# Two address homes for the streamed weight pieces of a fused hybrid layer

## The chip, the cores and the metric

The kernel runs on one core of one Trainium2 chip. The metric is the device time of one launch in microseconds. The profile, the trace and every row below come from one execution of the kernel, taken by the hardware profiler. The names of its engines are PE (TensorE matmul), PEld (TensorE weight load), DVE (VectorE), ACT (ScalarE), POOL (GpSimd) and SP (SyncE).

## The reference

One layer with 256 tokens of width 2048. A wide projection feeds four branches (a gated linear recurrence, dilated attention in three groups, RWKV-7, and a convolution with layer norm); their outputs are gated, projected back to width 2048, weighted by sigmoids of a fifth slice of the projection, summed, projected by `w_out`, added to the input and normalized.

```python
h = jnp.einsum('bsd,de->bse', x, w_in) + b_in
(a_x, a_gate, q, k, v, b_gate, c_r, c_k, c_v, c_wd, c_ad, c_gate,
 d_val, d_glu, d_gate, merge_logits) = jnp.split(h, split_points, axis=-1)
y_a = ...   # depthwise conv, block gates, linear scan
y_b = ...   # dilated window attention, 3 groups x 4 heads
y_c = ...   # RWKV-7 scan, 8 heads of 64
y_d = ...   # depthwise conv of 31 taps, layer norm, silu
merge_g = jax.nn.sigmoid(merge_logits).reshape(bsz, s, N_BRANCH, D_MODEL)
mixed = jnp.zeros_like(x)
for n in range(N_BRANCH):
    mixed = mixed + merge_g[:, :, n] * jnp.einsum('bsc,cd->bsd', ys[n] * jax.nn.silu(gates[n]), w_br[n])
out = jnp.einsum('bsd,de->bse', mixed, w_out)
return _layernorm(ALPHA * x + out, ln_g, ln_b)
```

All data is float32. The kernel splits each float32 operand of the large projections into two parts of the type float32r (`h`, and `l` for what is left) and adds three products: h by h, h by l and l by h.

## The kernel before, in words

The weights (w_in, w_br and w_out, some 185 MB) are streamed once, in pieces of 512 KB: 128 partitions by 1024 float32. `split` handles one piece. SyncE issues the load into a tile `raw`, ScalarE casts it to `wh` (L208), and VectorE computes `wl` = raw - wh (L209, shown in the trace as L65, the line of a helper that records VectorE's instructions). The cast and the subtraction are traced with a priority 400 instructions ahead of their place in the program. `raw` has four tiles, `wh` and `wl` have three each, all in the pool `wp`.

A piece is used in one of two ways. In `channel_major` and `opening`, `multiply` (L229) takes 128 columns of the piece as the stationary operand and moves 256 tokens of x; a piece gives 24 matmuls. In `token_major` (L279), 128 tokens of x (or of a gated branch output, or of the mixed sum) stand, and 512 columns of the piece move; a piece gives 12 matmuls (w_out's fourth chunk: 24 with 256 columns).

The two parts of x are `xh` and `xl` in the pool `xp`, which also holds the gated branch outputs `yh` and `yl`; later the tiles of xh and xl hold the two parts of the mixed sum. The pools are placed in address order as they are opened: `cp` (constants), `ap` (tags `mx4`, `tt`, `pad`), `wp`, `xp`, `bp` (all other tiles, with twelve tiles of the tag `rk`). The streamed weights thus lie directly below x. The last 256 columns of w_out are an exception: their parts `lasth` and `lastl` are `rk` tiles in `bp`, above x, and move over the standing mixed sum (L1056).

The order of the projections is fixed by the program: the opening, then channel-major up to the gate `ga` (to 182 us in the trace), token-major `merge(0)` (to 306), channel-major `gd`, token-major `merge(3)` (329 to 450), channel-major `gc`, q and k (to 626), token-major v, channel-major `gb` (692 to 717), then token-major to the end: `merge(2)`, `merge(1)`, w_out. Each change from one kind to the other is called a handover below; there are seven.

The branches are generators in the queue `side`; `pump` runs some of their steps after each piece, against a budget. Their VectorE instructions keep program order. The instructions of each engine are put in order by a scheduler when the program is built, and a tile waits for the release of the tile whose place it takes.

`tt` has five tiles. Its users are, in program order: u, th, gi, rd, rs (the linear recurrence), acc, sh, sl, csq, sh, sl (the convolution branch), the gates ga, gd, gc, gb, the outputs yc and yb, and at the end four tiles `z`, which GpSimd loads with x for the residual.

Of the kernel before, what the change touches and what calls it, by code (L numbers as in the profile page):

```python
# [19 lines left out]
P = 128  # L20
T = 256
# [52 lines left out]
def tile_hybrid(  # L74
# [8 lines left out]
    ap = ctx.enter_context(tc.tile_pool(name="ap", bufs=1))  # L83
    wp = ctx.enter_context(tc.tile_pool(name="wp", bufs=1))
    xp = ctx.enter_context(tc.tile_pool(name="xp", bufs=1))
    bp = ctx.enter_context(tc.tile_pool(name="bp", bufs=1))
    pss = ctx.enter_context(tc.tile_pool(name="pss", bufs=4, space=PSUM))
    psb = ctx.enter_context(tc.tile_pool(name="psb", bufs=4, space=PSUM))
# [2 lines left out]
    def big(tag, bufs, name, dt=F32):  # L91
        pool = ap if tag in ("mx4", "tt") else xp if tag in ("yh", "yl") else bp
        return pool.tile([P, NJ, T], dt, tag=tag, name=name, bufs=bufs)

    def tt(name, dt=F32):
        return big("tt", 5, name, dt)

    def rk(name, dt=F32):
        return big("rk", 12, name, dt)
# [99 lines left out]
        pump(1e12)  # L199


    def split(src, c0, n, k, nk, queue=None):
        raw = wp.tile([P, nk, n], F32, tag="raw", name="raw", bufs=4)
        (queue or nc.sync).dma_start(raw, src[:, k : k + nk, c0 : c0 + n])
        h = wp.tile([P, nk, n], F32R, tag="wh", name="wh", bufs=3)
        l = wp.tile([P, nk, n], F32R, tag="wl", name="wl", bufs=3)
        with tc.high_priority(offset=AHEAD):
            S.copy(h, raw)  # L208
            V.tensor_tensor(l, raw, h.bitcast(F32), op=ALU.subtract)  # L209
        return h, l  # L210
# [27 lines left out]
    def channel_major(src, nk, c0, n, rh, rl, budget):  # L238
        ps = columns(n)
        for k0, kn in pieces(nk, n):  # L240
            multiply(ps, *split(src, c0, n, k0, kn), k0, kn, nk, rh, rl)
            pump(budget * n * kn / (512 * KP))
        return ps

    def opening(cols, budget):

        pss_ = [columns(512) for _ in cols]
        for k0, kn in ((0, 1), (1, 1)) + tuple((k, KP) for k in range(2, KT, KP)):
            xs = load_x(k0, kn)
            for n, (c0, ps) in enumerate(zip(cols, pss_)):  # L250
                early = S if k0 < 2 and n == 0 else None
                if k0 == 0 and n == 0:
                    parts_ = [split(w_in_r, c0 + q * T, T, 0, 1, early) for q in range(2)]
                    split_x(xs, k0, kn)
                    for q, (h, l) in enumerate(parts_):
                        multiply(ps[0 : 2 * q + 2], h, l, 0, 1, KT, xh, xl, 2 * q)
                    continue
                h, l = split(w_in_r, c0, 512, k0, kn, early)
                if n == 0:
                    split_x(xs, k0, kn)  # L260
                multiply(ps, h, l, k0, kn, KT, xh, xl)
                pump(budget * kn / KP)
        return pss_
# [7 lines left out]
    def token_major(src, nk, c0, lh, ll, budget, n=512):  # L271
        ps = [pss.tile([P, 512], F32, tag="ps", name="ps") for _ in range(2)]
        for k0, kn in pieces(nk, n):
            h, l = split(src, c0, n, k0, kn)
            for t in range(2):
                for k in range(kn):
                    kk = k0 + k
                    for i, (a, w) in enumerate(((lh, h), (ll, h), (lh, l))):
                        PE.matmul(  # L279
                            ps[t][:, 0:n],  # L280
                            a(kk, t),
                            w[:, k, :],
                            start=(kk == 0 and i == 0),
                            stop=(kk == nk - 1 and i == 2),
                        )
            pump(budget * n * kn / (512 * KP))
        return ps
# [50 lines left out]
    def lru(ax, sps, res):  # L338
        (sp8,) = sps
        u = tt("u")  # L340
        for j in range(NJ):
            V.tensor_scalar(u[:, j, :], ax[:, j, :], col(PK_CONV + 3, j), col(PK_CONVB, j), op0=ALU.mult, op1=ALU.add)
            for back in range(1, 4):
                o = u[:, j, back:T]
                V.scalar_tensor_tensor(o, ax[:, j, 0 : T - back], col(PK_CONV + 3 - back, j), o, op0=ALU.mult, op1=ALU.add)
            yield 1300
        th = tt("th")
        gi = tt("gi")
        for j in range(NJ):
            ps = bank("psg")  # L350
            PE.matmul(ps[:, 0:T], bd[0][:, j, :], u[:, j, :], start=True, stop=True)
            PE.matmul(ps[:, T:], bd[1][:, j, :], u[:, j, :], start=False, stop=True, skip_group_check=True)
            S.activation(th[:, j, :], ps[:, 0:T], AF.Sigmoid, bias=col(PK_GAB, j))
            S.activation(gi[:, j, :], ps[:, T:], AF.Sigmoid, bias=col(PK_GXB, j))
            yield 0
        rd = tt("rd")
        rs = tt("rs")
        for j in range(NJ):
            V.tensor_scalar(th[:, j, :], th[:, j, :], sp8[:, j : j + 1], None, op0=ALU.mult)
        yield 800  # L360
        S.activation(rd, th, AF.Exp, scale=-1.0)
        S.activation(th, th, AF.Tanh, scale=0.5)
        V.tensor_scalar(rd, rd, 0.5, 0.5, op0=ALU.mult, op1=ALU.add)
        V.scalar_tensor_tensor(rs, th, 1.0, rd, op0=ALU.add, op1=ALU.mult)
        yield 1700
        V.scalar_tensor_tensor(rd, rs, 2.0, rd, op0=ALU.subtract, op1=ALU.mult)
        yield 1100
        V.tensor_scalar(rs, th, 1e-33, None, op0=ALU.max)
        S.activation(rs, rs, AF.Sqrt)
        V.tensor_tensor(u, gi, u, op=ALU.mult)  # L370
        yield 1700
        V.scalar_tensor_tensor(th, th, 1e17, rs, op0=ALU.mult, op1=ALU.min)
        yield 1100
        V.scalar_tensor_tensor(th, th, -2.0, rd, op0=ALU.mult, op1=ALU.mult)
        yield 1100
        V.tensor_tensor(u, u, th, op=ALU.mult)
        yield 1100
        V.tensor_scalar(rd, rd, -2.0, -1.0, op0=ALU.mult, op1=ALU.add)
        yield 600
        y = gi  # L380
        for j in range(NJ):
            V.tensor_tensor_scan(y[:, j, :], rd[:, j, :], u[:, j, :], 0.0, ALU.mult, ALU.add)
        yield 1400
        res.append(y)
# [13 lines left out]
    def conformer(cu, res):  # L398
        acc = tt("acc")
        for w in range(31):  # L400
            for j in range(NJ):
                if w == 0:
                    V.tensor_scalar(acc[:, j, :], cu[:, j, 0:T], col(PK_DW, j), col(PK_DWB, j), op0=ALU.mult, op1=ALU.add)
                else:
                    V.scalar_tensor_tensor(
                        acc[:, j, :], cu[:, j, w : w + T], col(PK_DW + w, j), acc[:, j, :], op0=ALU.mult, op1=ALU.add
                    )
                yield 400
        ps = bank("psm")
        total(ps, parts(acc, tt))  # L410
        mean = bp.tile([P, T], F32, tag="s1", name="mean", bufs=4)
        S.activation(mean, ps[:, 0:T], AF.Copy, scale=1.0 / BW)
        V.tensor_tensor(acc, acc, mean[:, None, :].to_broadcast([P, NJ, T]), op=ALU.subtract)
        sq = tt("csq")
        S.activation(sq, acc, AF.Square)
        yield 1100
        ps = bank("psv")
        total(ps, parts(sq, tt))
        rstd = bp.tile([P, T], F32, tag="s1", name="rstd", bufs=4)
        S.activation(rstd, ps[:, 0:T], AF.Sqrt, bias=eps_ln, scale=1.0 / BW)  # L420
        V.reciprocal(rstd, rstd)
        V.tensor_tensor(acc, acc, rstd[:, None, :].to_broadcast([P, NJ, T]), op=ALU.mult)
        yield 1500
        for j in range(NJ):
            S.activation(sq[:, j, :], acc[:, j, :], AF.Sigmoid, bias=col(PK_CB, j), scale=col(PK_CG, j))
            V.tensor_scalar(acc[:, j, :], acc[:, j, :], col(PK_CG, j), col(PK_CB, j), op0=ALU.mult, op1=ALU.add)
        V.tensor_tensor(acc, acc, sq, op=ALU.mult)
        yield 1900
        res.append(acc)
# [528 lines left out]
    merge(1, *yhb, False, True)  # L958


    z = [[tt("z").rearrange("p a b -> p (a b)") for _ in range(2)] for _ in range(2)]
    for t in range(2):
        for i in range(2):
            G.dma_start(z[t][i], x[t * P : (t + 1) * P, i * 1024 : (i + 1) * 1024])
# [77 lines left out]
        for t in range(2):  # L1042
            residual(t, i, c0, n, ps[t])
    for k in range(0, KT, 4):
        raw = wp.tile([P, 4, T], F32, tag="raw", name="raw", bufs=4)
        nc.sync.dma_start(raw, w_out_r[:, k : k + 4, DM - T :])
        S.copy(lasth[k // 4], raw)
        V.tensor_tensor(lastl[k // 4], raw, lasth[k // 4].bitcast(F32), op=ALU.subtract)
# [98 lines left out]
```

## Time and profile before

| what | value |
| --- | --- |
| three runs | 1057.39, 1058.17, 1058.19 us; median 1058.17 us |
| the profiled execution, its own time | 1057.35 us |
| span from its first to its last instruction | 1055.6 us |
| TensorE busy | 1042.8 us |
| VectorE busy | 722.2 us |
| ScalarE busy | 497.0 us |
| mean granted TensorE clock | 0.995 |
| read from HBM | 198.98 MB |

The span is what the trace covers; the execution's own time has 1.75 us more around it. Busy time of TensorE counts pipelined matmuls with modelled ends, so the pace of a stream is better read from how long a run of so many matmuls takes in the chain of waits. That chain goes back from the last instruction, at each step to what released it or to the instruction before it on its engine.

### The profile page before, as it was taken

What the parts mean: (1) busy time and instruction counts of PE and PEld (TensorE: products, weight loads), DVE (VectorE), ACT (ScalarE), POOL (GpSimd) and SP (SyncE); (2) the same over time, 40 slices, a digit from 0 to 9 for tenths busy, and PEclk for the clock granted to TensorE, in tenths of its full rate; (3) what the DMA queues carried; (4) which work ended last, traced back from release to release, by engine and by line L of the source; (5) the groups of instructions that cost most, each with busy time, mean ns of one, the idle gap of its engine ahead of it and who ended that gap; (6) DMA issues with size and microseconds to landing.
All of it is one profiled execution on the core that took longest, in us unless ns stands there. A gap on an engine that the chain in (4) does not pass through costs nothing.

```text
span 1055.6 us, 16618 instructions
## 1 busy us (share of the span) xinstructions
PE 1042.8 (99%) x6669; PEld 921.2 (87%) x6669; DVE 722.2 (68%) x985; ACT 497.0 (47%) x594; POOL 41.4 (4%) x75
## 2 busy tenths in 40 slices
PE   7999999999999999999999999999999999999997
PEld 6999999887789877899999998898888888888886
DVE  5769988999969996665544444556666565556656
ACT  3365445557734435434544443346565444345341
POOL 0010000000020020000100000000000000000000
PEclk9999999999999999999999999999999999999998
DMA  8885766665686677555866666664556667676662
GB/s 279 247 254 155 204 187 186 189 183 150 186 215 187 199 206 200 182 154 151 288 180 181 182 187 189 194 183 142 170 154 209 209 202 206 207 226 199 193 192 89
DMA packets 108174, 203.11 MB, mean 192 GB/s; under 512 B 8436, under 2 KB 17296, under 8 KB 108096
## 3 DMA queue, kind: packets, MB, share of 16 engines
q1 hardware_dynamic: 102160, 185.16, 58.9%
q0 software_dynamic: 4928, 15.30, 5.0%
q10 hardware_dynamic: 1008, 1.57, 0.4%
q8 instruction: 52, 0.85, 0.3%
q14 instruction: 26, 0.21, 0.1%
HBM read 198.98 MB, written 5.39 MB: 194 GB/s over the span
## 4 chain that ended last, share of the span: by engine, by line
PE 93%; DVE 3%; DMA 2%; issue 1%; ACT 0%; SPq 0%; DVEq 0%; POOL 0%
PE ps L279 50%; PE ps L229 36%; DVE xw L65 1%; DVE wl L65 1%; PE ps L1056 1%; DMA raw<-in_w_in 1%; DMA x<-scr 1%; PE psl L803 1%; DMA xt<-scr 1%; DVE z L65 0%; PE po L827 0%; PE pab L580 0%; PE pm L872 0%; PE py L736 0%; PE pu L699 0%
## 5 line engine op out<-in xcount | busy, mean ns | idle before, releaser
L65 DVE TENSOR_TENSOR wl<-raw,wh 128x1024 fp32r<-128x1024 f32 (+1 forms) x345 | 417.7, 1213 | 275.5 <-ACT wh L208 274.2
L208 ACT CAST wh<-raw 128x1024 fp32r<-128x1024 f32 (+1 forms) x345 | 358.9, 1043 | 470.4 <-PE ps L279 240.7
L229 PE MATMUL ps<-xh,wh 128*128 128x256 f32 x1040 | 295.2, 285 | 4.3 <-ACT wh L208 4.3
L229 PE MATMUL ps<-xl,wh 128*128 128x256 f32 x1040 | 294.1, 284 | 0.0
L229 PE MATMUL ps<-xh,wl 128*128 128x256 f32 x1040 | 291.7, 285 | 0.0
L279 PE MATMUL ps<-wh,xh 128*128 128x512 f32 x608 | 237.9, 391 | 0.0
L279 PE MATMUL ps<-wh,xl 128*128 128x512 f32 x608 | 237.2, 390 | 0.0
L279 PE MATMUL ps<-wl,xh 128*128 128x512 f32 x608 | 221.0, 393 | 0.5 <-DVE wl L65 0.5
L229 PEld LDWEIGHTS ps<-xh,wh 128*128 128x128 f32 x1040 | 199.1, 191 | 5.8 <-ACT wh L208 4.5
L229 PEld LDWEIGHTS ps<-xl,wh 128*128 128x128 f32 x1040 | 199.1, 191 | 0.3
L229 PEld LDWEIGHTS ps<-xh,wl 128*128 128x128 f32 x1040 | 196.9, 191 | 0.7 <-DVE wl L65 0.2
L279 PEld LDWEIGHTS ps<-wl,xh 128*128 128x128 f32 x608 | 114.1, 188 | 26.4 <-DVE wl L65 1.6
L279 PEld LDWEIGHTS ps<-wh,xl 128*128 128x128 f32 x608 | 114.1, 188 | 23.9 <-issue 0.3
L279 PEld LDWEIGHTS ps<-wh,xh 128*128 128x128 f32 x608 | 114.2, 188 | 23.2 <-ACT wh L208 0.3
L65 DVE SCALAR_TENSOR_TENSOR acc<-cu,pkt,acc 128x256 f32<-128x256 f32 x120 | 50.7, 481 | 0.0
L279 PE MATMUL ps<-wh,ml 128*128 128x512 f32 (+1 forms) x128 | 46.5, 364 | 0.0
L279 PE MATMUL ps<-wh,mh 128*128 128x512 f32 (+1 forms) x128 | 46.3, 363 | 0.0
L279 PE MATMUL ps<-wl,mh 128*128 128x512 f32 (+1 forms) x128 | 43.0, 364 | 0.0
L842 POOL DMA_DIRECT2D bm<-in_b_row x16 | 8.8, 551 | 653.1 <-DVE mg L65 625.0
L279 PEld LDWEIGHTS ps<-wh,mh 128*128 128x128 f32 x128 | 24.2, 189 | 3.8
L279 PEld LDWEIGHTS ps<-wh,ml 128*128 128x128 f32 x128 | 24.2, 189 | 3.7
L279 PEld LDWEIGHTS ps<-wl,mh 128*128 128x128 f32 x128 | 24.0, 189 | 3.7
(319 smaller groups left out, 885.5 us busy)
## 6 DMA issues: line engine op xcount, KB each, us to landing
raw<-in_w_in SPq DMA_DIRECT2D x280, 512.0 KB, 4.0
raw<-in_w_br SPq DMA_DIRECT2D x32, 512.0 KB, 4.5
raw<-in_w_out SPq DMA_DIRECT2D x32, 512.0 KB, 4.7
bm<-in_b_row POOLq DMA_DIRECT2D x16, 256.0 KB, 4.3
fscr<-frow POOLq DMA_DIRECT2D x3, 768.0 KB, 7.7
z<-in_x POOLq DMA_DIRECT2D x4, 512.0 KB, 6.6
xs<-in_x_t SPq DMA_DIRECT2D x7, 256.0 KB, 8.1
hb<-fscr POOLq DMA_DIRECT2D x3, 512.0 KB, 4.4
```

The costliest lines, as they stand in the source:

```text
L65: ins = f(*a, **k)
L208: S.copy(h, raw)
L229: PE.matmul(ps[j], w[:, k, (j - j0) * P : (j - j0 + 1) * P], r[:, kk, :], start=(kk == 0 and i == 0 and j % 2 == 0), stop=(kk == nk - 1 an ...
L279: PE.matmul(ps[t][:, 0:n], a(kk, t), w[:, k, :], start=(kk == 0 and i == 0), stop=(kk == nk - 1 and i == 2),)
L803: PE.matmul(ps[:, 0:w], qt[g][:, h, q * P : (q + 1) * P], kt[g][:, h, 0:w], start=True, stop=True)
L842: G.dma_start(bias, row(b_row[c0 : c0 + 512]))
L1056: PE.matmul(ps[:, 0:T], mix(a)(k, t), w[k // 4][:, k % 4, :], start=(k == 0 and i == 0), stop=(k == KT - 1 and i == 2))
```

## The change

The pool `wp` (below x) and a new pool `wq` (above x) get one tag each, `wa` and `wb`, with six tiles of 4 KB per partition. The new pool is opened after `xp` and before `bp`. A function `piece` picks the pool. `channel_major` and `opening` call `split` with `False`, `token_major` with `True`. `split` is told whether the weights move: their two parts then go below x, and the raw piece above it; where they stand, the parts go above x and the raw piece below it. The raw pieces of w_out's last 256 columns go above x.

`tt` shrinks from five tiles to three. rd, rs, csq and the split sums sh and sl (in all seven allocations) take `rk` tiles instead, and the fourth `z` tile takes the place of `yh`.

```diff
+    wq = ctx.enter_context(tc.tile_pool(name="wq", bufs=1))
...
-        return big("tt", 5, name, dt)
+        return big("tt", 3, name, dt)
...
-    def split(src, c0, n, k, nk, queue=None):
-        raw = wp.tile([P, nk, n], F32, tag="raw", name="raw", bufs=4)
+    def piece(below, nk, n, name, dt=F32):
+        return (wp if below else wq).tile([P, nk, n], dt, tag="wa" if below else "wb", name=name, bufs=6)
+
+    def split(src, c0, n, k, nk, moves, queue=None):
+        raw = piece(not moves, nk, n, "raw")
         (queue or nc.sync).dma_start(raw, src[:, k : k + nk, c0 : c0 + n])
-        h = wp.tile([P, nk, n], F32R, tag="wh", name="wh", bufs=3)
-        l = wp.tile([P, nk, n], F32R, tag="wl", name="wl", bufs=3)
+        h, l = piece(moves, nk, n, "wh", F32R), piece(moves, nk, n, "wl", F32R)
...
-            multiply(ps, *split(src, c0, n, k0, kn), k0, kn, nk, rh, rl)
+            multiply(ps, *split(src, c0, n, k0, kn, False), k0, kn, nk, rh, rl)
...
-            h, l = split(src, c0, n, k0, kn)
+            h, l = split(src, c0, n, k0, kn, True)
...
-        rd = tt("rd")
-        rs = tt("rs")
+        rd = rk("rd")
+        rs = rk("rs")
...
-        total(ps, parts(acc, tt))
+        total(ps, parts(acc, rk))
...
-        sq = tt("csq")
+        sq = rk("csq")
...
-        total(ps, parts(sq, tt))
+        total(ps, parts(sq, rk))
...
-    z = [[tt("z").rearrange("p a b -> p (a b)") for _ in range(2)] for _ in range(2)]
+    z = [tt("z"), tt("z"), tt("z"), big("yh", 1, "z")]
+    z = [[z[2 * t + i].rearrange("p a b -> p (a b)") for i in range(2)] for t in range(2)]
...
     for k in range(0, KT, 4):
-        raw = wp.tile([P, 4, T], F32, tag="raw", name="raw", bufs=4)
+        raw = piece(False, 4, T, "raw")
```

## Rows read from the trace of the kernel before

**Rows 1.** The page's first part: busy time, share of span, instructions by engine.
```profile
PE 1042.8 (99%) x6669; PEld 921.2 (87%) x6669; DVE 722.2 (68%) x985; ACT 497.0 (47%) x594; POOL 41.4 (4%) x75
```

**Rows 2.** Costliest groups: busy us, mean ns of one | idle us before, releaser.
```profile
L65 DVE TENSOR_TENSOR wl<-raw,wh 128x1024 fp32r<-128x1024 f32 (+1 forms) x345 | 417.7, 1213 | 275.5 <-ACT wh L208 274.2
L208 ACT CAST wh<-raw 128x1024 fp32r<-128x1024 f32 (+1 forms) x345 | 358.9, 1043 | 470.4 <-PE ps L279 240.7
L229 PE MATMUL ps<-xh,wh 128*128 128x256 f32 x1040 | 295.2, 285 | 4.3 <-ACT wh L208 4.3
L279 PE MATMUL ps<-wh,xh 128*128 128x512 f32 x608 | 237.9, 391 | 0.0
```

**Rows 3.** Chain of waits in order of time: start us, us, what.
```profile
1.65 8.49 DMA raw<-in_w_in
...
75.89 106.55 PE ps L229 x888
182.44 25.42 PE ps L279 x112
...
306.12 23.03 PE ps L229 x192
329.16 16.36 PE ps L279 x72
...
450.56 3.54 PE ps L229 x28
...
626.07 3.65 PE ps L279 x16
...
646.80 45.39 PE ps L279 x200
692.19 14.27 PE ps L229 x119
...
746.55 1.29 PE po L827 x6
...
1028.38 5.28 PE ps L279 x44
1033.66 10.69 PE ps L1056 x89
```

**Rows 4.** Busy time by stretch: length, busy per engine, clock, DMA share, GB/s.
```profile
0.00:20.00 20.00, 14.44 (x83) 11.90 (x84) 11.04 (x24) 7.14 (x10) 2.47 (x8) 0.91 0.83 254
...
329.00:450.00 121.00, 119.69 (x743) 97.21 (x743) 99.29 (x134) 56.79 (x72) 10.36 (x18) 1.00 0.68 194
```

**Rows 5.** Waits of SyncE's queue: total us, times, longest us.
```profile
SPq L204 <- DVE wl L65: 657.1, 264, 7.5
```

**Rows 6.** ScalarE's timeline around six handovers: start us, us, what [idle before].
```profile
176.59 1.05 ACT L208 CAST wh<-raw 128x1024 fp32r<-128x1024 f32 x1 [1.83 <-PE ps L229]
...
180.54 1.28 ACT L299 ACT_TABLE_LOAD   x1
...
300.49 1.06 ACT L208 CAST wh<-raw 128x1024 fp32r<-128x1024 f32 x1 [2.97 <-PE ps L279]
...
323.31 1.05 ACT L208 CAST wh<-raw 128x1024 fp32r<-128x1024 f32 x1 [1.82 <-PE ps L229]
...
442.46 1.05 ACT L208 CAST wh<-raw 128x1024 fp32r<-128x1024 f32 x1 [1.70 <-PE ps L279]
...
620.23 1.05 ACT L208 CAST wh<-raw 128x1024 fp32r<-128x1024 f32 x1 [1.83 <-PE ps L229]
...
686.56 1.05 ACT L208 CAST wh<-raw 128x1024 fp32r<-128x1024 f32 x1 [1.67 <-PE ps L279]
```

**Rows 7.** The tile raw, whole span and then 640 to 690 us.
```profile
DMA to landing us min/median/max: 2.8/4.2/10.7
...
DMA to landing us min/median/max: 3.5/3.7/3.8
```

**Rows 8.** VectorE's timeline near 329 us: start us, us, what.
```profile
326.43 1.22 DVE L65 TENSOR_TENSOR wl<-raw,wh 128x1024 fp32r<-128x1024 f32 x1
```

**Rows 9.** GpSimd's timeline, 800 to 812 us: start us, us, what [idle before].
```profile
805.61 0.55 POOL L964 DMA_DIRECT2D z<-in_x  x1 [15.57 <-DVE gb L65]
```

More of the change, by code (lines that the diff above doesn't have):

```diff
@@ L252, in opening @@
                 if k0 == 0 and n == 0:
-                    parts_ = [split(w_in_r, c0 + q * T, T, 0, 1, early) for q in range(2)]
+                    parts_ = [split(w_in_r, c0 + q * T, T, 0, 1, False, early) for q in range(2)]
                     split_x(xs, k0, kn)
@@ L257, in opening @@
                     continue
-                h, l = split(w_in_r, c0, 512, k0, kn, early)
+                h, l = split(w_in_r, c0, 512, k0, kn, False, early)
                 if n == 0:
```

## The prediction

> **What bounds the kernel now.** I read the page's busy shares first, then the groups by line, the chain of waits, busy time by stage, and last the timelines where one kind of projection hands over to the other. TensorE is busy for 1042.8 of the 1055.6 us [rows 1], so only two things can move the time: the pace of its matmuls, or new gaps between them. The stream is 3120 channel-major matmuls (L229, three groups of 1040: weights stand, x moves, 256 columns) and the token-major ones (L279: x stands, weights move, 512 columns). ACT's cast to wh and DVE's subtraction to wl take 1.04 and 1.21 us a piece, and sat idle for 470 and 275 us in total before them: they wait for others, and PE waits for a cast only in the opening, 4.3 us [rows 2].
>
> The pace is in the chain, where long runs of one line give it without any modelled end: 106.55 us for 888 L229 matmuls is 120.0 ns each, and 45.39 us for 200 at L279 is 227.0 [rows 3]. PE's granted clock is 1.00 in these stretches, for example from 329 to 450 us [rows 4], so it is at its 2.4 GHz level, where 256 columns take 106.7 ns and 512 take 213.3. Every matmul of the stream thus costs some 13.3 ns more than its columns, whatever their number. The fp32 matmuls of attention (po) run at 215 ns for 256 columns [rows 3], twice 106.7 and only 2 more: the surplus belongs to the stream, not to every matmul.
>
> **What the change does, part by part.** *1. Placement.* The addresses of weights and x change. The trace already has three placements with 256 columns: weights standing below x with x moving (75.89 us on, 120.0 ns), x standing with weights moving from just below it (w_out's fourth chunk, 5.28 us for 44: 120.0 ns), and x standing with weights moving from above it (lasth and lastl in the last pool, L1056, 10.69 us for 89: 120.1 ns) [rows 3]. Order and distance do not show at all. Weights standing above x, which 3120 matmuls get, is the one placement with no row. I price it by the three that have one: 0. The bounds: at best the whole surplus but po's 2 ns goes, 3120 x 11 ns = 34 us. On the other side the three rows leave at most some 0.1 ns, 0.3 us.
>
> The Trainium skill ("TensorE: Matmul & The Clock Gate", Part 1, the section on 56 against 53.3 ns) puts the warm spacing at N/2.4 plus about 2.5 ns; by it L229 would run at 109 ns, and the trace's 120.0 disagrees. The same page (Part 2, step by step, LDWEIGHTS) gives PE two independent SBUF read ports, so that loading weights takes nothing from the running matmul; by that rule placement is worth nothing, as the three rows say.
>
> *2. Two rings of six in place of raw 4, wh 3, wl 3.* Within one kind of projection little changes: three pairs of h and l as before, and six raws instead of four. Today SyncE waits for a raw slot 264 times for DVE's subtraction, 657 us in all [rows 5]: loads are early and only wait for a slot. Deeper raws can save at most what PE idles in the middle of the kernel, 121.00 - 119.69 = 1.3 us in the stretch 329 to 450 [rows 4]. There the late thing is DVE's subtraction, not the load, so I take 0.
>
> *3. Handovers.* This is the new wait. A token-major raw lives in the ring that holds the h and l of channel-major pieces, and the other way round. Just before a handover all six tiles are taken by the h and l of the last three pieces, so the first raw of the new kind can be loaded only when PE has finished the third-last piece. Today that event starts the cast of the first new piece, since the cast waits for the same release while its raw has long landed: at 176.59, 300.49, 323.31, 442.46, 620.23 and 686.56 us [rows 6]. PE comes to the new kind at 182.44, 306.12, 329.16, before 450.56, 626.07 and 692.19 [rows 3]. That leaves 5.85, 5.63, 5.85, about 8, 5.84 and 5.63 us. The seventh, near 717, has attention's small matmuls in its last two pieces, as the one at 450 has rwkv's; these two I count as covered.
>
> In that window must now fit: about 0.1 us to the issue, the landing, 0.1 to the cast, 1.05 for the cast [rows 6] and 1.23 for the subtraction. A raw lands 4.2 us after its issue in the median, 3.7 where loads come one at a time (640 to 690 us) [rows 7]. Here two are issued together (h and l come free together) onto idle queues, so I take 4.0. Then h is ready after 5.25 us, in time everywhere, and l after 6.5. PE needs l at its third matmul, two spacings into the piece: 0.45 us (token-major) or 0.24 us (channel-major) after the window. The stalls: 6.5 - 5.85 - 0.45 = 0.2 at 182, the same at 626; 6.5 - 5.63 - 0.24 = 0.63 at 306 and at 692. At 329 the subtraction today starts at 326.43, 2.07 us after its cast ended (323.31 + 1.05), because DVE is working through rwkv's xw chain [rows 8]; the slack that now absorbs this is gone, so 0.2 + 2.07 = 2.3. Sum 0.2 + 0.63 + 2.3 + 0.2 + 0.63 = 4.0 us.
>
> Bounds: 0 if a load gets one of the two slots a piece earlier (2.9 us more). At the other end the two loads share the queues to the end: 0.52 MB at the 254 GB/s that the first 20 us moved [rows 4] takes 2.1 us, so 3.7 + 2.1 = 5.8, which is 1.8 more at each of five, 13 us in all. What is queued behind a late piece: on SP only later raws; on ACT the evacuations (at 182 a table load and ga's sigmoids come right then [rows 6]), which free banks that PE wants two chunks later; on DVE the side work, which has slack until its `finish`. After the first piece the loads run ahead again, since a piece's PE time (2.7 to 2.9 us) exceeds 2.1 us.
>
> *4. The opening.* The first loads are shared as they are: a raw issued at 1.65 us takes 8.49 us to land and PE waits for it [rows 3]. Six slots let two more raws (1.05 MB, 4.1 us at 254 GB/s) go out beside it, or let raws go ahead of x pieces needed later. Between +4.1 and about -1.5 us, I take 0.
>
> *5. tt from 5 to 3, and its users in rk; z's last quarter in yh.* No instruction is added. rd, rs, csq and the split sums take rk slots, of which 12 exist, while only blocks, ax and the rwkv inputs live; u, th, gi fit the three tt slots, and acc, ga, gd, gc, yb, gb follow with at most three alive. The z loads move from earlier slots: today the last is issued at 805.61 behind gb [rows 9], now two wait for yb and gb and one for yh's last reader in w_br. From there to its use lie two or more w_out chunks of 96 x 0.227 = 21.8 us, against a worst landing of 10.7 [rows 7]. It costs 0 while that cover stands; without it, its landing, up to 10.7 us.
>
> Sum: 4.0 us. The profiled execution took 1057.35 us, 1.75 of it outside the span; with 4.0 that is 1061.4. The median of the runs is 0.8 above it, so 1062.2, say 1062.
>
> **The rivals.**
> *Faster: the surplus is a collision of PE's two reads that the new home of standing weights removes.* Its place is L229 alone. For it: the surplus is per matmul, po lacks it, and this placement is untried. Against: three placements, 120.0, 120.0 and 120.1 ns [rows 3]. It decides from 1.3 ns a matmul, where 3120 matmuls pay the 4.0 us of stalls; a quarter of the surplus gives 1062 - 8.6 = 1053, all of it 1062 - 34 = 1028. By the spacing rule of the Trainium skill's TensorE page this last case would be the normal one.
> *No difference: the loads get slots early enough, or land in 3.5 us.* With one of the two freed tiles going to the raw a piece earlier the window grows by 2.9 us, and even 329 is covered: 1058.2. For it: order in a ring isn't visible in this trace. Against: h and l stand before the raw in program order.
> *Slower by more: the opening.* Two more loads beside the first ones delay the raw that PE waits for; at the full 4.1 us on top, 1066.
>
> **How the numbers follow.** A measurement of this kernel tells some 0.2%, 2.1 us, from no change. Handover stalls between 2.2 and 10 us: 0.40, time 1062, own range 1060 to 1068. Stalls hidden or below 2 us, nothing else: 0.30. Cheaper standing matmuls: 0.25, spread from 1055 down to 1024, about half of it below 1046. The slow opening: 0.05. So faster 0.25, same 0.30, slower 0.45. The range reaches from 1046, which leaves out about 0.12 of the cheap end, to 1068, which leaves about 0.06.
>
> **What would show it.** In the chain after: L229 at 120 ns and L279 at 227 says placement is nothing; 118 or less says the faster rival. At 182, 306, 329, 626 and 692 us: the first new raw issued no earlier than about 5.7 us before PE's switch, and PE idle behind wh or wl. The first switch of all, PE's run from 10.8 us on, tells of the opening. I am wrong if the pace of L229 moves, or if the raw at a handover is issued earlier than the third-last piece's end.

## The result, and the profile after

The changed kernel takes 1064.22 us (median of 4 runs, 1063.42 to 1066.67), the kernel before, on the same chip, 1058.04 (1057.39 to 1058.19): a ratio of 1.0067 with a 95% interval of 1.0055 to 1.0080, so 0.67% slower. The forecast said 1062, inside 1046 to 1068, slower with a chance of 0.45. Its mechanism came out as written, but its sum did not: of 6.5 us lost in the span (1055.6 to 1062.1) the stalls that it priced, 4.0 us, were 1.5 to 1.8, and the rest came by ways that it had held to be free.

The page of the kernel after (busy us, mean ns of one | idle before, releaser), against [rows 1, 2]:

```profile
PE 1045.5 (98%) x6669; PEld 921.5 (87%) x6669; DVE 721.0 (68%) x985; ACT 495.2 (47%) x593; POOL 41.4 (4%) x75
...
L282 PE MATMUL ps<-wh,xh 128*128 128x512 f32 x608 | 238.1, 392 | 1.3 <-ACT wh L211 1.3
```

L229 of before is L232 now, L279 is L282, L1056 is L1060. The instructions are the same but for one activation-table load of ScalarE that is gone (593 in place of 594), and TensorE's and VectorE's take what they took: this token-major group's matmul has a mean of 392 ns in place of 391. Token-major matmuls now wait 1.3 us for casts where they had waited 0.0.

The chain of waits (start us, us, what), against [rows 3]:

```profile
75.08 106.55 PE ps L232 x888
181.63 31.00 PE ps L282 x136
...
692.86 3.81 DMA raw<-in_w_in
696.70 1.06 ACT wh L211
697.78 1.24 DVE wl L65
699.06 19.70 PE ps L232 x162
...
816.93 66.68 PE ps L282 x294
```

106.55 us for 888 matmuls: the placement that had no row costs 120.0 ns, to the last digit what it cost in the other home. 66.68 for 294 token-major matmuls is 226.8 ns each. The pace is untouched, so the loss is made of gaps. The four rows from 692.86 on show the new wait as forecast: the raw piece is issued when TensorE ends the third-last piece, lands, is cast and subtracted, and TensorE is released at 699.06, with no work of the old kind left to hide it.

Where the time was lost is read from when TensorE reaches each stage. At 182 us it is 0.8 us ahead of before (181.63; the opening moved 303 GB/s in its first 20 us, not 254). The token-major stage that began at 329.16 [rows 3] begins at 334.47, 5.3 us behind. So 6.1 us are lost between these points, in the first merge and in gd; from there to the last matmul of the stream (1044.06 us before, 1051.51 after) it is 2.1 more, and the tail behind it gives 1.0 back. Of the 2.1, 1.1 is a side matmul (pp) that waits 1.9 us for a transfer of x from scratch memory where it had waited 0.8, 0.25 the handover at 699, and 0.7 a subtraction that comes late at 1031 us, in w_out.

TensorE's waits from 45 to 1020 us (total us, times, longest), before and then after:

```profile
PE pp L639 <- DMA x<-scr: 0.8, 1, 0.8
PE ps L279 <- DVE wl L65: 0.5, 1, 0.5
```

```profile
PE pp L642 <- DMA x<-scr: 1.9, 1, 1.9
PE ps L282 <- ACT wh L211: 1.3, 2, 1.0
PE ps L232 <- DVE al L65: 0.8, 1, 0.8
PE ps L282 <- DVE wl L65: 0.7, 2, 0.4
PE ps L232 <- DVE wl L65: 0.7, 2, 0.4
```

Waits are counted from modelled ends and so come out short; I count a gap as the time between two starts less the usual 120 or 227 ns. From 182 to 334 us that gives five losses:

| at, us | us lost | what it is |
|---|---|---|
| 236 to 241 | 1.95 | evacuation and subtraction late on VectorE, behind side work |
| 292 to 300 | 1.5 | rwkv's small matmuls pab and pak: four blocks of 1.13 us each before, 5.97 together after |
| 309 | 0.5 | a handover |
| 321 to 325 | 1.4 | subtractions at 320.07 and 324.20 that wait for their casts, and these for landings; the second is what the view puts down to al |
| 334 | 0.7 | a handover |

Together they are 6.05 of the 6.1. Three of the five are not at a handover.

**The handover at 329 us**, where the forecast had its largest term. SyncE issues the raw pieces from 328.30 on; ScalarE's, VectorE's and TensorE's timelines of after show what follows (start us, us, what [idle before, releaser]):

```profile
333.37 1.05 ACT L211 CAST wh<-raw 128x1024 fp32r<-128x1024 f32 x1 [6.57 <-DMA raw<-in_w_in]
```

```profile
334.45 1.23 DVE L65 TENSOR_TENSOR wl<-raw,wh 128x1024 fp32r<-128x1024 f32 x1 [0.96 <-ACT wh L211]
```

```profile
334.47 0.50 PE L282 MATMUL ps<-wh,xh 128*128 128x512 f32 x1 [0.33 <-ACT wh L211]
```

The cast starts 5.07 us after the issue and waits for the landing alone. All that stands in front of this subtraction in VectorE's order was done by then, and the engine sat idle for 0.96 us; the rest of the xw chain comes behind it (from 335.59). The 2.07 us queue of the forecast isn't there.

**236 to 241 us**, 54 us after a handover. The chain of after:

```profile
230.44 4.82 PE ps L282 x22
235.25 1.14 DVE wl L65
236.39 0.40 DVE d L65
236.79 1.66 DVE rstd L65
238.45 0.33 DVE wa L65 x2
238.78 0.10 DVE mg L65
...
239.30 0.68 DVE mg L65
239.98 1.14 DVE wl L65
241.16 3.92 PE ps L282 x16
```

No load is in this chain. VectorE is busy throughout, and the subtraction that TensorE needs at 241.16 stands in its order behind side work (d, rstd, wa) and behind mg, the evacuation of a bank of results. The view of waits puts the longest wait here (1.0 us, up to 239.53) down to a cast that ended just before; the first half of mg ended then too, and it frees the bank that the next chunk writes. Which of the two held TensorE isn't shown; neither waited for a load. In the kernel with rings held by role, below, three subtractions stand between rstd and mg, here none. Its timeline of VectorE:

```profile
227.08 1.74 DVE L65 RECIPROCAL rstd<-rstd 128x256 f32<-128x256 f32 x1
228.74 1.16 DVE L65 TENSOR_TENSOR wl<-raw,wh 128x1024 fp32r<-128x1024 f32 x1
...
230.21 1.21 DVE L65 TENSOR_TENSOR wl<-raw,wh 128x1024 fp32r<-128x1024 f32 x1
...
234.06 1.22 DVE L65 TENSOR_TENSOR wl<-raw,wh 128x1024 fp32r<-128x1024 f32 x1
...
235.59 1.28 DVE L65 TENSOR_TENSOR mg<-ps,bm 128x512 f32<-128x512 f32 x2
```

**303 to 325 us**. The tile raw as issued in 295 to 325 us, before and then after (who waited: us, times; landing):

```profile
L204 SPq DMA_DIRECT2D raw<-in_w_in x10: 367/368/368, 294.8 to 324.9; - x10
...
  ACT wh L208: 2.1, 1
...
DMA to landing us min/median/max: 3.8/4.9/9.8
```

```profile
L208 SPq DMA_DIRECT2D raw<-in_w_in x8: 368/395/697, 303.0 to 311.8; - x8
...
  ACT wh L211: 12.7, 8
...
DMA to landing us min/median/max: 4.1/8.4/13.9
```

Before, ten loads go out over 30 us, and ScalarE once waits for one. After, eight go out within 9 us, together with the al transfers (issued 309.4 to 311.8, landing after 9.3 us in the median), and land in up to 13.9; ScalarE waits for all eight. The lead that the old order had stored up is what is gone.

### The profile page after: what moved, and what is told of

The parts are those of the page before. It is cut to its first block, busy times and chain, and to the rows that moved or that the text cites. A ratio compares the mean times of both kernels' runs of the same rounds, so it can differ in the third digit from the quotient of the medians.

```text
span 1062.1 us, 16599 instructions
## 1 busy us (share of the span) xinstructions
PE 1045.5 (98%) x6669; PEld 921.5 (87%) x6669; DVE 721.0 (68%) x985; ACT 495.2 (47%) x593; POOL 41.4 (4%) x75
## 4 chain that ended last, share of the span: by engine, by line
PE 84%; issue 9%; DMA 4%; DVE 2%; ACT 1%; POOL 1%; ACTq 0%; DVEq 0%; POOLq 0%
PE ps L282 44%; PE ps L232 32%; DMA raw<-in_w_in 1%; PE ps L1060 1%; DVE wl L65 1%; DMA x<-scr 1%; PE psl L806 1%; DMA raw<-in_w_out 1%; DMA scr<-ab 0%; DVE z L65 0%; PE po L830 0%; DMA scr<-xw 0%; ACT wh L211 0%; DMA xt<-scr 0%; PE pm L875 0%
## 5 line engine op out<-in xcount | busy, mean ns | idle before, releaser
L211 ACT CAST wh<-raw 128x1024 fp32r<-128x1024 f32 (+1 forms) x345 | 359.4, 1043 | 473.1 <-PE ps L282 228.9
L232 PE MATMUL ps<-xh,wh 128*128 128x256 f32 x1040 | 293.7, 284 | 3.1 <-ACT wh L211 2.7
L232 PE MATMUL ps<-xl,wh 128*128 128x256 f32 x1040 | 293.3, 284 | 0.5 <-DVE xl L65 0.5
L232 PE MATMUL ps<-xh,wl 128*128 128x256 f32 x1040 | 289.4, 284 | 2.1 <-DVE wl L65 1.2
L282 PE MATMUL ps<-wh,xh 128*128 128x512 f32 x608 | 238.1, 392 | 1.3 <-ACT wh L211 1.3
L282 PE MATMUL ps<-wh,xl 128*128 128x512 f32 x608 | 237.4, 391 | 0.0
L282 PE MATMUL ps<-wl,xh 128*128 128x512 f32 x608 | 220.3, 393 | 0.8 <-DVE wl L65 0.7
L232 PEld LDWEIGHTS ps<-xh,wh 128*128 128x128 f32 x1040 | 198.2, 191 | 5.0 <-ACT wh L211 3.1
L232 PEld LDWEIGHTS ps<-xl,wh 128*128 128x128 f32 x1040 | 198.3, 191 | 1.1 <-DVE xl L65 0.7
L232 PEld LDWEIGHTS ps<-xh,wl 128*128 128x128 f32 x1040 | 195.7, 191 | 3.6 <-DVE wl L65 3.3
L282 PEld LDWEIGHTS ps<-wl,xh 128*128 128x128 f32 x608 | 114.1, 188 | 27.1 <-DVE wl L65 2.5
L282 PEld LDWEIGHTS ps<-wh,xh 128*128 128x128 f32 x608 | 114.2, 188 | 25.4 <-ACT wh L211 1.9
L282 PEld LDWEIGHTS ps<-wh,xl 128*128 128x128 f32 x608 | 114.2, 188 | 23.5 <-issue 0.2
L282 PE MATMUL ps<-wh,ml 128*128 128x512 f32 (+1 forms) x128 | 46.5, 364 | 0.0
L282 PE MATMUL ps<-wh,mh 128*128 128x512 f32 (+1 forms) x128 | 46.2, 363 | 0.0
L282 PE MATMUL ps<-wl,mh 128*128 128x512 f32 (+1 forms) x128 | 42.9, 364 | 0.5 <-DVE wl L65 0.5
L282 PEld LDWEIGHTS ps<-wl,mh 128*128 128x128 f32 x128 | 23.9, 189 | 4.3 <-DVE wl L65 0.7
L282 PEld LDWEIGHTS ps<-wh,mh 128*128 128x128 f32 x128 | 24.2, 189 | 3.8
L282 PEld LDWEIGHTS ps<-wh,ml 128*128 128x128 f32 x128 | 24.2, 189 | 3.7
```

The lines of the kernel that those rows point to most:

```text
L232: PE.matmul(ps[j], w[:, k, (j - j0) * P : (j - j0 + 1) * P], r[:, kk, :], start=(kk == 0 and i == 0 and j % 2 == 0), stop=(kk == nk - 1 an ...
L282: PE.matmul(ps[t][:, 0:n], a(kk, t), w[:, k, :], start=(kk == 0 and i == 0), stop=(kk == nk - 1 and i == 2),)
```

## The experiments

Times are ratios to the kernel before in the same group of runs (its medians there: 1056.65, 1057.14 and 1057.91 us), each with its 95% interval.

### Addresses alone

```diff
     wp = ctx.enter_context(tc.tile_pool(name="wp", bufs=1))
+    wq = ctx.enter_context(tc.tile_pool(name="wq", bufs=1))
     xp = ctx.enter_context(tc.tile_pool(name="xp", bufs=1))
-    wq = ctx.enter_context(tc.tile_pool(name="wq", bufs=1))
```

> The changed kernel with the second ring of pieces opened right after the first, so that both lie below x; the order of the instructions on every engine stays that of the changed kernel, only addresses differ. Placement does nothing (my theory): 1064 us, within 2 us of the changed kernel, the 888 channel-major matmuls of the chain again 106.55 us (120.0 ns each). Placement works (rival): the standing weights go back below x, so that if their place above x had cost or saved anything the 120.0 or 227 ns per matmul move by at least 1 ns, which over 4,000 matmuls is 4 us or more.

1066.29 us, ratio 1.0082 (1.0067 to 1.0098). The changed kernel's is 1.0067 (1.0055 to 1.0080): the intervals overlap, and on VectorE, ScalarE and TensorE the two traces have the same instructions in the same order. Its chain:

```profile
77.16 106.55 PE ps L232 x888
```

Placement is nothing that can be told, for weights that stand below or above x: 120.0 ns either way. That agrees with the rule of the Trainium skill that the forecast named (TensorE: Matmul & The Clock Gate, Part 2: two independent read ports).

### The same rings, held by role

```diff
-        raw = piece(not moves, nk, n, "raw")
+        raw = piece(True, nk, n, "raw")
-        h, l = piece(moves, nk, n, "wh", F32R), piece(moves, nk, n, "wl", F32R)
+        h, l = piece(False, nk, n, "wh", F32R), piece(False, nk, n, "wl", F32R)
```

(the raw of lasth follows; the mirror has False and True the other way round)

> The changed kernel with the rings held by role: raw pieces always in the ring below x, both parts always in the ring above x, six slots each, so no ring changes hands when the stream changes between channel-major and token-major. Handover theory: the first raw piece after a change is issued some 20 us ahead of TensorE as in the steady stream, not 5.5 to 7.3 us; the stalls that follow the changes (about 1.5 us in all) and the two behind the gd change (0.49 and 0.91 us at 320 to 325) go, 1061 us or a little less, 1059 to 1062. Rival, the order: the lost time comes from the order into which the side work fell when the pieces' pools and the tt tiles changed; then this stays at 1064 as far as that order is kept, or moves by gaps elsewhere than at the changes.

> The mirror of the run with raw pieces always below x: raw pieces always above x, both parts always below x, six slots each; the order of instructions is the same on every engine in the two. Handover theory and no effect of placement: 1061 us, equal to its mirror within 1 us. Placement rival: the two differ, since here both parts have the addresses below x for either use and there the ones above.

1057.38 us, ratio 1.0008 (0.9999 to 1.0017), and 1056.98, ratio 1.0001 (0.9991 to 1.0010). Both are level with the kernel before, and with each other. So the exchange of the rings carries the whole loss, 6 to 7 us, twice what I expected of it. All five losses are gone; from 45 to 1020 us the view of waits shows a single one of TensorE, 1.0 us, for a side matmul. The tile raw in 295 to 325 us:

```profile
L208 SPq DMA_DIRECT2D raw<-in_w_in x10: 367/368/368, 294.6 to 323.5; - x10
...
DMA to landing us min/median/max: 3.6/4.8/8.1
```

My rival, the order of the engines, is not refuted: with no exchange the order too is another, and this pair can't part them.

### The tt part alone, and six raw slots without an exchange

```diff
-        return (wp if below else wq).tile([P, nk, n], dt, tag="wa" if below else "wb", name=name, bufs=6)
+        return wp.tile([P, nk, n], dt, tag=name, name=name, bufs=4 if name == "raw" else 3)
```

(second kernel: 6 for 4; wq is dropped in both)

> The kernel before with one part of the change alone: tt cut from 5 to 3 tiles, rd, rs, the parts of the channel sums and csq in rk tiles, and the fourth z in the tile of yh; the pieces keep their pools of before (4 raw, 3 and 3 parts). My price of zero for this part: 1058 us, within 1 us. Rival: the tiles' other homes move the side work (the parts of the sums wait for rk tiles), and the part carries the 2 us of stalls at 235 to 240 and the longer side blocks of the changed kernel (2.3 us): 1060 to 1062.

> The tt part with pools by role as in the kernel before (raw, first part, second part, all below x), but six raw slots in place of four. Handover theory: nothing is shared between raw pieces and parts, so no stall; like the two runs with roles, whose instruction order it has on most engines: 1055 to 1058 us, the same as before or faster by up to 2 us through the opening, whose loads are issued as early as in the changed kernel. Rival, a deeper load queue by itself disturbs the stream (side transfers queue behind raw pieces): over 1060.

1056.04 us, ratio 0.9993 (0.9980 to 1.0005), and 1056.89, ratio 1.0000 (0.9992 to 1.0009). Both of my prices of zero hold: fewer tt tiles cost nothing, six raw slots bring nothing. No version here beats the kernel before.

### The exchange in one stretch at a time

The kernel with roles, whose token-major pieces exchange the rings only in the first merge (shown), only in the merge after gd, or only from the values on (in the first two the raw of lasth is as with roles):

```diff
+    swap = [False]
...
-            h, l = split(src, c0, n, k0, kn, True)
+            h, l = split(src, c0, n, k0, kn, swap[0])
...
+    swap[0] = True
     merge(0, *yha, True, False)
+    swap[0] = False
```

> The run with roles (raw always below x, parts always above) with the rings changing hands for one stretch alone, the first merge, at 182 us into it and at 306 us out of it. Between those two points the changed kernel lost 3.1 us on the run with roles, and 2.9 us more in the channel-major stretch of gd behind the second. Theory: two changes carry that by themselves, through their waits and through the order that the build laid around them: 6 us over the run with roles, 1061 to 1064 us. Rival, only the stalls directly at a change cost: 0 at 182 us and 0.5 at 306 us, 1057 to 1058 us.

> The run with roles with the rings changing hands for the merge that follows gd alone, at 329 us into it and at 450 us out of it. The changed kernel stalls 0.7 us behind the first and none behind the second, and lost 3 us between 329 and 510 us in all. Theory, waits and order: 1 to 3 us over the run with roles, 1058 to 1060. Rival, the direct stalls alone: 1058.

> The run with roles with the rings changing hands for the last three changes alone (values at 626 us, back at 692 us, and again at 717 us to the end). The changed kernel stalls 0.25 us at 698 us and 0.66 us at 1031 us and is otherwise level with the run with roles in these stretches. Theory: under 1 us over the run with roles, 1057 to 1058.5. Rival, the changes share the loss evenly: three of seven, 4 us, 1061.

| exchanged | handovers at | us | ratio, 95% interval |
|---|---|---|---|
| first merge | 182, 306 | 1064.30 | 1.0071 (1.0056 to 1.0087) |
| merge after gd | 329, 450 | 1058.88 | 1.0019 (1.0008 to 1.0029) |
| from the values on | 626, 692, 717 | 1057.40 | 0.9998 (0.9986 to 1.0011) |

The first merge alone loses as much as the changed kernel, though its direct stalls are nil and 0.5 us. The merge after gd costs some 2 us, as expected. The three handovers from the values on cost nothing that can be told. The rivals "only direct stalls count" (1057 to 1058 for the first merge) and "the changes share the loss evenly" (1061 for the last) both fall.

### One handover at a time

With placement worth nothing, the rings can be exchanged once and stay so. The kernel with roles, turned before the first merge (182; shown), before gd (306) or before the merge after it (329). In their traces L232 is L235, L282 is L285 and L211 is L214.

```diff
+    turned = [False]
...
+        moves = turned[0]
         raw = piece(not moves, nk, n, "raw")
...
+    turned[0] = True
     merge(0, *yha, True, False)
```

> The run with roles (raw below x, parts above) whose rings change hands once, before the first merge at 182 us, and stay so to the end. Theory: the direct stall at this change is nil (the changed kernel shows none), but the build, which lays the order of the engines out on a simulated timeline, moves VectorE's side work so that second parts come late at 236 to 241 us: 1.9 us of stalls there, 2 to 3 us over the run with roles in all, 1059 to 1060.5. Rival, the loss of the first merge all comes from the change at its end: 1057, and no stall at 236 to 241 us.

> The same with the one change before gd, at 306 us. Theory: the stall behind the change (0.5 us) and the ones at 321 to 325 us, where the raw pieces, issued only a few us ahead, meet the small packets of the al transfer (1.4 to 2.1 us): 2 to 3 us over the run with roles, 1059 to 1060.5. Rival, the first merge's loss all comes from the change into it: 1057 to 1057.5, with no stall at 321 to 325 us.

> The same with the one change before the merge that follows gd, at 329 us. By my forecast 2.3 us of stall behind it; by the changed kernel's trace 0.7 us, and in the run with this one merge turned 0.3 us, with 1.2 us at 385 to 388 us. Theory: 1 to 2 us over the run with roles, 1058 to 1059.5; rival (the forecast's queue behind VectorE's side chain): 1059.5 or more, with over 1.5 us of stall within 8 us of the change.

1062.14 us, ratio 1.0044 (1.0028 to 1.0061); 1062.54, ratio 1.0050 (1.0031 to 1.0070); 1058.32, ratio 1.0010 (0.9999 to 1.0021). Either handover of the first merge costs by itself more than I expected, and not in the same way.

*At 182*: TensorE's waits in 225 to 245 us, then 303 to 340, and VectorE's timeline at the latter:

```profile
PE ps L285 <- ACT wh L214: 1.0, 1, 1.0
PE ps L285 <- DVE wl L65: 0.4, 1, 0.4
...
PE ps L235 <- DVE wl L65: 1.1, 1, 1.1
```

```profile
319.62 0.09 DVE L65 MEMSET al<- 128x32 f32 x1 [4.68 <-DMA al<-scr]
321.31 0.19 DVE L65 TENSOR_TENSOR xw<-al,xw 128x32 f32<-128x32 f32 x1 [1.61 <-DMA xw<-in_cst]
321.45 1.23 DVE L65 TENSOR_TENSOR wl<-raw,wh 128x1024 fp32r<-128x1024 f32 x1
```

No stall at the handover, then the stalls of the changed kernel at 236 to 241 to the digit, and one more at 321 us, 15 us after the point where no exchange happens here. There a subtraction stands behind side work that waits for the al and xw transfers; the pieces' loads are on time. In the kernel with roles the first xw step starts at 314.30, here at 321.31, 7.0 us later, while TensorE reaches gd only 4.0 us later (309.68 against 305.65): the xw transfer was issued 4.4 us later and took 10.0 us to land where it had taken 7.4. So my rival, all from the change at the end, falls, and so does my reading that stalls at 321 us need a handover at 306.

*At 306*: TensorE's waits from 303 to 340 us, and the tile raw in 295 to 325:

```profile
PE ps L235 <- DVE wl L65: 1.9, 3, 0.8
PE ps L235 <- ACT wh L214: 0.6, 1, 0.6
```

```profile
  ACT wh L214: 12.8, 7
...
DMA to landing us min/median/max: 4.2/9.1/14.0
```

Here TensorE has before the handover only the wait of 1.0 us that the kernel with roles has too, pab and pak alternate as there, and the cost is the bunched loads: 0.6 us of gap at the handover and 2.65 at 315 to 320. The trace is of an execution of 1059.98 us, the shortest of seven that reach 1067.13, so these gaps don't account for the whole of the median's loss.

*At 329*: 0.5 us of gap behind it, 1.2 at 385 to 387; the time is within 0.21% of the kernel before. The forecast's stall of 2.3 us isn't there.

**The order on the engines.** The traces settle what moves it. By operation and tile, VectorE's 985 instructions stand in one order in the kernel with roles and its mirror, and in another in the changed kernel; the two part at the 258th, at 183.06 us, right behind the first handover. The kernels that exchange at 182 us (the first merge alone, the change at 182) follow the changed kernel to 299 us at least and have its losses at 236 to 241 us. Those that first exchange later follow the kernel with roles: VectorE leaves its order at 304.68 us in the change at 306, at 316 us in the two that begin at 329, at 691 us in the one that begins with the values at 626. They don't have these losses; instead they wait there 1.0 us for a side matmul, as it does. On ScalarE and TensorE the orders too part near each kernel's first exchange. So the exchange changes the order, and not only the waits.

### Four handovers inside the first merge

```diff
+    turned = [False]
...
+        moves = turned[0]
...
         for c in range(4):
+            turned[0] = n == 0 and c % 2 == 0
             c0 = C_M + n * DM + c * 512
...
-        raw = piece(False, 4, T, "raw")
+        raw = piece(True, 4, T, "raw")
```

> The run with roles with four changes inside the first merge: the rings turned for its first and third quarter (at 182, 213, 244 and 275 us), and none at 306 us. Theory: each change costs the lead of the raw pieces (5 to 7 us in place of 20) and 0 to 0.7 us of direct stall, and an order of its own: 2 to 5 us over the run with roles, 1059 to 1062, and no stall at 321 to 325 us, where the lead is whole. Rival, a change costs nothing by itself and only the one at 306 us counts: 1057.

1064.55 us, ratio 1.0068 (1.0051 to 1.0084): above the range that I gave. TensorE's waits from 180 to 340 us:

```profile
PE ps L285 <- DVE wl L65: 1.7, 2, 0.9
PE ps L285 <- ACT wh L214: 0.8, 1, 0.8
```

Again next to nothing at 182 (0.2 us at 189), 2.1 us of gaps at 238 to 243, 1.4 at 279 to 283, and none at 303 to 340, where the lead is whole. The last two lie around the third and the fourth handover, whose first raw pieces are issued at 235.59 and 270.64. Four handovers cost as much as the two at 182 and 306: what counts is what each meets, not their number.

## Why the forecast was right, and where it wasn't

1. *Placement*: right, 120.0 ns in the fourth placement, and two pairs of kernels that differ by addresses are level. The faster rival (0.25) is dead, and with it the part of the range below 1057.
2. *Two rings of six*: zero, right, by the two kernels with roles, which hold two rings of six, and by the run with six raw slots. SyncE still waits for VectorE's subtraction, 620.9 us in 229 waits, in place of [rows 5].
3. *Handovers*: the mechanism is right. The first raw piece of the new kind is issued 5.5 to 7.3 us before TensorE needs it at all seven, and the cast follows 3.8 to 4.1 us after the issue (5.07 at 329), against 4.1 assumed. The size of the direct stalls was not: at 182, 306, 329, 626 and 692 us they were nil, 0.5, 0.7, at most 0.3, and 0.25 us, 1.5 to 1.8 in all, not 4.0. Most of the excess is the 2.07 us for VectorE's queue at 329: that queue was read from a timeline in which the subtraction came earlier; here all that stands in front of it was done 0.96 us before it could start.
4. The step that failed is the sentence "After the first piece the loads run ahead again", and beside it "on DVE the side work, which has slack". At gd the loads did not run ahead: eight bunched into 9 us beside small transfers, a burst that the old lead had covered. And the handover moves side work on VectorE and TensorE in front of pieces that were on time. The order in which a kernel's instructions stand on each engine is laid out at its build. That it is the exchange that brings this order is shown: the orders part where the first exchange stands. By what rule the build reacts to the new waits is not shown. Of the 6.05 us, 2.6 (309, 321 to 325 and 334 us) end with a piece whose cast had waited for its landing, and 3.4 (236 to 241 us, pab and pak) with work in another order and no load. That is a division by what ended each gap; a kernel with the new waits in the old order, or the reverse, was not tried, so what either would cost alone stays open.
5. *The opening*: -0.8 us at 182 us, inside its bounds (+4.1 to -1.5). *tt, rk, z*: zero, right.

So the total fell within 2.2 us of the forecast by luck: an overcount (4.0 for some 1.7) and an omission (nearly 5 us) met. The rival "no difference" failed at its reason, a slot freed a piece earlier: that did not happen once in seven.

## What to carry to other kernels

When two kinds of buffer exchange places in one ring, the newcomer waits for the last reader of the other kind, and the price can be less the stall at that point (here 1.5 to 1.8 us of 6.5) than the lost lead and the changed order: look for the next burst of transfers and the next side chain that the lead used to cover. Rings held by role need the same bytes and had no such point here. A forecast that moves a wait in a kernel whose order is planned at build must also allow for another order, and should ask where an in-order engine has critical work that could slip behind side work.

## What the runs showed of the hardware

Interleaving of small matmuls matters. In the chain of before, pab and pak (64x64 weights, 128 columns) alternate, and a block of 32 takes 1.04 us, from the start of its first matmul to that of the next of the stream:

```profile
292.64 0.25 PE pab L580
...
293.68 2.99 PE ps L279 x12
```

In the chain of after, 16 of one alone take as long:

```profile
294.91 1.02 PE pab L583 x16
...
296.36 1.02 PE pak L584 x16
```

And while the al transfers land, the DMA engines are busy without moving much. In 295 to 325 us of after:

```profile
DMA  3600063550029599998899999999999998999620
GB/s 66 109 22 0 0 115 60 87 87 0 0 38 126 167 399 418 412 205 101 232 380 377 391 401 388 197 188 186 186 191 150 197 172 218 317 374 388 251 109 25
```

Each digit is 0.75 us: from 314 to 320 us the engines are nine tenths busy at 150 to 218 GB/s, where just before, at the same share, they moved 377 to 401. In these 30 us 351 packets were under 512 bytes; that they are the reason is likely, but no run here parts them from the rest.
